# Attention of a hybrid layer: scores with the keys on the partitions, row maxima taken in a pass of their own and fed in as constant rows

## The chip, the cores and the metric

The kernel runs on one core of one Trainium2 chip. The metric is device time in microseconds (us). A core has five engines that work side by side, each through its own list of instructions in a fixed order: PE (TensorE, matrix products and transposes), DVE (VectorE), ACT (ScalarE), POOL (GpSimd) and SP (SyncE, which here only starts DMA transfers). An engine that waits for one instruction holds up everything behind it in its list.

## What is computed

One layer of a streaming encoder on a prompt of 1024 tokens and a block of 32 sample tokens, width 1024. The input is projected, half of the mixing width goes through a state-space branch (S5), the other half through latent attention (MLA) with 8 heads, and both halves meet in one output projection. The part that the change touches:

```python
def mla_attend(q_nope, q_rope, k_nope, k_rope, v, mask):
    s = jnp.einsum('bqhn,bkhn->bhqk', q_nope, k_nope) + jnp.einsum('bqhr,bkr->bhqk', q_rope, k_rope)
    s = s.astype(jnp.float32) * (NOPE_DIM + ROPE_DIM) ** -0.5
    if mask is not None:
        s = jnp.where(mask, s, -jnp.inf)
    pr = jax.nn.softmax(s, axis=-1)
    return jnp.einsum('bhqk,bkhv->bqhv', pr.astype(v.dtype), v)
...
    mix = jnp.concatenate([rmsnorm(y_ssm, p['out_norm_ssm']) * jax.nn.silu(g_ssm),
                           rmsnorm(attn, p['out_norm_mla']) * jax.nn.silu(g_mla)], axis=-1)
    return x + mix @ p['w_out'], ckv, krope, h_last
```

Query q sees key k where the chunk (64 tokens) of q is not before that of k. A head has 64+32 score channels and 64 value channels.

## The kernel before

**Stages.** (1) Input projection (`mt`, L235) with the token norms; (2) the state-space branch; (3) its gate (`gl`); (4) expansion of queries and keys/values for the first four heads (`q_p`, L797 to L799; `kv_p`, L765 to L767); (5) attention; (6) output projection. A scheduler fixes each engine's order when the program is built, from a simulated time line; a tile in a pool of buffers may be written only when the buffer's last reader has gone, so the number of buffers takes part in that order.

**Output projection.** `half(base, ...)` (L855) multiplies one half of the mixed channels by four 128-row blocks of `wout`. Each block is loaded into `wor`, which has two buffers, by a DMA on ACT's queue; `hilo` makes two parts of it, `woh` (ACT) and `wol` (DVE, L113); and the raw block also serves the sample tokens' product `wos` (L863). So the third block's transfer waits until `wos` has read the first. Then each tile of 128 tokens takes 24 products `wo` (L873), 128x512 each: 2 column halves, 4 blocks, 3 parts; 192 for a half. `half(0)` (state-space channels; `out_ssm`, ACT, L885) is a generator that the attention's preamble steps through; `half(4)` (attention channels; `out_y`, DVE, L1184) comes last. `wo` and `wos` take PSUM buffers of tag "w", `q_p`, `kv_p`, the transposes and the value sums those of tag "b" (4).

**Attention.** Heads go in four pairs p; for each pair, 8 query tiles i of 128 (32 units u). `q_tr` transposes the queries, `prep` the keys (`kt_p`). `scores` (L980 to L982) makes [queries on partitions x keys] in three passes (high x high, high x low, low x high); DVE takes the maximum of each row (L989, L1002), ACT the exponential with that as bias and the row sum as accumulated output (L992, L1004). `trans` turns the exponentials into [keys x queries], 128x128 at a time on PE (`pt_p`, L1020, 288 of them); DVE or ACT copies them out of PSUM (L1024, L1026). `values` (L1048) multiplies with the values, 288 products of 128 query columns, each two instructions; the two heads of a pair write two 64-row halves of one PSUM tile. The reciprocal row sums (L1040) are spread by POOL (`rle`, L1042) and transposed by PE (L1049, 32). `finish_at` (POOL) gates, squares and splits the result into `ath` and `atl`. Mask: 8 extra contraction rows, 96 to 103.

**Norms.** `rsqrt` (L151 to L160) is a chain of 11 small DVE instructions; it serves the input norm (`rst`, whose row form `rb` comes out of PE transposes `rb_p`, L185, and scales `uT` at L251), the two branch norms, and the q and kv norms.

Of the kernel before, what the change touches and what calls it, by code (L numbers as in the profile page):

```python
# [24 lines left out]
NT = NP_ + NS  # L25
# [25 lines left out]
def step(ctx: ExitStack, tc, xT, xr, winF, winT, wuq, wukv, wglu, wout, ckvcT, krcT, pk, rot, ssb, ssc, mtab,  # L51
         y_o, ckv_o, kr_o, st_o, dbg=None):
    nc = tc.nc
    pe, act, dve, pool, sp = nc.tensor, nc.scalar, nc.vector, nc.gpsimd, nc.sync

# [106 lines left out]

    def col_rstd(ss, which, name):
# [11 lines left out]
        marks[name] = rsqrt(r, ms, TS)  # L175
# [110 lines left out]
    marks["rst"] = rsqrt(rst, ssx, TS)  # L286
# [568 lines left out]
    def half(base, mix, smp, rstd, out, after, eng=sp):  # L855
        ww = []
        ps = PA("wos", "w")
# [7 lines left out]
        for i0 in range(0, 8, 2):  # L865
            s = {i: [PA("wo", "w") for _ in range(2)] for i in (i0, i0 + 1)}
            mm = {i: mix(i * 128, 128) for i in s}
            for kr in ((0, 1, 2), (3,)) if i0 == 0 else ((0, 1, 2, 3),):
                for i in s:
                    for c in range(2):  # L870
                        for k in kr:
                            for a, b, first, last in ((0, 0, True, False), (0, 1, False, False), (1, 0, False, True)):
                                pe.matmul(s[i][c], mm[i][a][k], ww[k][b][:, c * 512:(c + 1) * 512],  # L873
                                          start=(k == 0 and first), stop=(k == 3 and last))
            if i0 == 0:
                rs = rstd()
                dve.scalar_tensor_tensor(ysm, ps[:, :256], rs[:, 8:9], ysm, op0=MUL, op1=ADD)
            for i in s:
                out(i, s[i], rs[:, i:i + 1])
            yield i0  # L880
# [23 lines left out]

    kT = {}
    KT = {}
    qTh = T("qTh", [104, 10, 256], 1, F32R)
    mk = [T("sg", [128, 1024], 2) for _ in range(2)]
    for j in range(2):
        with tc.issue_after(marks["qe", 0]):  # L910
            act.dma_start(mk[j][96:104], mtab[:, j])
    with tc.issue_after(marks["qe", 1]):
        act.activation(qTh[96:104, 0:8].rearrange("p i (j c) -> p i j c", j=2),
                       mk[0][96:104].rearrange("p (i c) -> p i c", c=128)[:, :, None, :].to_broadcast([8, 8, 2, 128]), AF.Copy)
# [5 lines left out]
    evac = [0]  # L920

    def prep(p, part):
# [3 lines left out]
        if p < 2 and part == 0:  # L926
            KT[p] = T("kTh", [104, 2, 2, 512], 2, F32R), T("kTl", [96, 2, 2, 512], 2, F32R)
        h, lo = (t[:, part] for t in KT[p % 2])
        kT[p, part] = (h, lo)
        if p < 2:  # L930
            src = krT[64:96, None, part * 512:(part + 1) * 512].to_broadcast([DR, 2, 512])
            split(h[64:96], lo[64:96], src, None,  ("qe", 1))
            with tc.issue_after(marks["qe", 1]):
                act.activation(h[96:104], mk[1][96:104, None, part * 512:(part + 1) * 512].to_broadcast([8, 2, 512]), AF.Copy)
# [23 lines left out]
    QT, PR, PTT, RL, OB = {}, {}, {}, {}, {}  # L958

    def q_tr(u):  # L960
        p, i = ORD[u]
# [4 lines left out]
        qh, ql = qTh[:, i], qTh[:96, 8 + u % 2]  # L966
        split(qh[:96], ql, pp[:96, :256], gqk[:96])
        QT[u] = (qh, ql)

    def scores(u):  # L970
        p, i = ORD[u]
        qh, ql = QT.pop(u)
        nb = i + 1
        rl = RL[u] = SM("rl", [4], bufs=4)

        def mm(s, j, c):
            n = min(512, nb * 128 - 512 * c)
            kh, kl = kT[p, c]
            qj = slice(j * 128, (j + 1) * 128)
            pe.matmul(s[:, :n], qh[:, qj], kh[:, j, :n], start=True, stop=False)  # L980
            pe.matmul(s[:, :n], qh[:96, qj], kl[:, j, :n], start=False, stop=False)  # L981
            pe.matmul(s[:, :n], ql[:, qj], kh[:96, j, :n], start=False, stop=True)  # L982

        n = nb * 128
        if i < 4:
# [3 lines left out]
            dve.tensor_reduce(rl[:, 2:4], s[:, :, :n], AX.X, ALU.max, negate=True)  # L989
            t = T("P", [128, 1024], 4)  # L990
            for j in range(2):
                marks["exp", u] = act.activation(t[:, j * n:(j + 1) * n], s[:, j, :n], AF.Exp,  # L992
                                                 bias=rl[:, 2 + j:3 + j], accum_out=rl[:, j:j + 1]).ins
            PR[u] = [t]
        else:
            PR[u] = []
            for j in range(2):
                s = PS2("S")
                for c in range(2):
                    mm(s[:, c], j, c)  # L1000
                sf = s.rearrange("p a b -> p (a b)")[:, :n]
                dve.tensor_reduce(rl[:, 2 + j:3 + j], sf, AX.X, ALU.max, negate=True)  # L1002
                t = T("P", [128, 1024], 4)
                marks["exp", u] = act.activation(t[:, :n], sf, AF.Exp, bias=rl[:, 2 + j:3 + j],  # L1004
                                                 accum_out=rl[:, j:j + 1]).ins
                PR[u].append(t)

    def trans(u):
        p, i = ORD[u]
        nb = i + 1  # L1010
        pr = PR.pop(u)
        out = []
        n = 2 * nb if i < 4 else nb
        for t in pr:
            o = T("PT", [128, 8, 128], 4)
            for b in range(0, n, 4):
                e = min(n, b + 4)
                pp = PA("pt_p", "b")
                for q in range(b, e):
                    pe.transpose(pp[:, (q - b) * 128:(q - b + 1) * 128], t[:, q * 128:(q + 1) * 128], ident)  # L1020
                ov = o[:, b:e].rearrange("p a b -> p (a b)")
                evac[0] += 1
                if evac[0] % 2:
                    dve.tensor_copy(ov, pp[:, :(e - b) * 128])  # L1024
                else:
                    act.activation(ov, pp[:, :(e - b) * 128], AF.Copy)  # L1026
            out.append(o)
        PTT[u] = [(out[0], 0), (out[0], nb)] if i < 4 else [(o, 0) for o in out]

    def values(u):  # L1030
        p, i = ORD[u]
        hf, c0 = p // 2, (p % 2) * 128
        nb = i + 1
        if u % 2 == 0:
            OB[p] = PA("ob", "b")
        ob = OB[p]
        r0 = (i // 4) * 128
        pt = PTT.pop(u)
        rl = RL.pop(u)
        dve.reciprocal(rl[:, 0:2], rl[:, 0:2])  # L1040
        re = T("rle", [128, 128], 2)
        pool.tensor_scalar(re.rearrange("p (a b) -> p a b", a=2), rl[:, 0:2, None].to_broadcast([128, 2, 64]),  # L1042
                           1.0, 0.0, op0=MUL, op1=ADD)
        for q in range(nb):
            for j in range(2):
                v = KV["p", q, hf][:, 256 + c0 + 64 * j:256 + c0 + 64 * j + 64]
                t, b = pt[j]
                pe.matmul(ob[64 * j:64 * j + 64, r0:r0 + 128], v, t[:, b + q], start=(q == 0), stop=(q == nb - 1))  # L1048
        pe.transpose(ob[:, 256 + r0:384 + r0], re, ident)  # L1049
        if u % 2:  # L1050
            bs = T("bs", [128, 256], 2)
# [280 lines left out]
```

## Time and profile before

| what | us |
|---|---|
| three runs | 583.57, 585.41, 587.38 (median 585.41) |
| the profiled execution, its own time | 584.77 |
| its span, first to last instruction | 583.0 |
| around the span (the difference) | 1.77 |
| PE busy | 547.1 (94%) |
| DVE busy | 414.8 (71%) |
| ACT busy | 304.4 (52%) |
| POOL busy | 107.5 (18%) |
| stages: (1) to (3) / (4) / (5), wo mixed in / rest of (6) | 0 to 287 / 287 to 348 / 348 to 540 / 540 to 583 |

PE is nearly always at work, but a stage can have another limit: the profile's table by stretches of time, the chain of work that ended last, and the groups of instructions by line show which. Matmuls overlap, so the price of one is read from the distance between starts, not from its own duration.

### The profile page before, as it was taken

The page shows a single profiled execution, that of the slowest core. Times are in us where ns is not written, and L with a number is a line of the kernel's source. Part 1 is how long each engine was busy: PE and PEld are TensorE (multiplying, and loading weights), DVE is VectorE, ACT ScalarE, POOL GpSimd, SP SyncE. Part 2 cuts the span into 40 slices and gives each one's busy share as a digit, 9 for nine tenths or more (in the row PEclk, how much of TensorE's full clock was granted, in tenths as well). Part 3 has the DMA queues.
Part 4 walks back from the last instruction along what each step waited for, and adds up shares of the span by engine and source line. Part 5 has one row for each costly group of instructions (what it writes and reads, how often), then busy time and mean ns, then how long its engine had stood idle before and what let it go on. Part 6 is the DMA issues. An engine that isn't in the chain of part 4 may idle for free.

```text
span 583.0 us, 9939 instructions
## 1 busy us (share of the span) xinstructions
PE 547.1 (94%) x3707; PEld 481.5 (83%) x3707; DVE 414.8 (71%) x1000; ACT 304.4 (52%) x673; POOL 107.5 (18%) x165
## 2 busy tenths in 40 slices
PE   5989699999999997599999799999999999999997
PEld 5989599899999996599788578877778888877885
DVE  6999722989999254129989986668798577683722
ACT  5571155218135247639855966776676775752000
POOL 0000000000000010000024520222244334468330
PEclk9999799999999998889999899999999999999799
DMA  8991752232433204632401121200100101095352
GB/s 286 405 304 41 199 136 92 49 143 89 130 97 103 66 18 154 201 100 90 141 17 61 43 91 74 92 2 1 38 20 2 38 3 38 7 373 200 104 230 108
DMA packets 35266, 63.92 MB, mean 110 GB/s; under 512 B 5361, under 2 KB 21521, under 8 KB 35217
## 3 DMA queue, kind: packets, MB, share of 16 engines
q1 hardware_dynamic: 31008, 49.06, 25.9%
q10 hardware_dynamic: 4208, 14.22, 6.9%
q8 instruction: 29, 0.48, 0.3%
q14 instruction: 21, 0.16, 0.1%
HBM read 47.06 MB, written 16.21 MB: 109 GB/s over the span
## 4 chain that ended last, share of the span: by engine, by line
PE 74%; DVE 10%; ACT 5%; DMA 5%; issue 2%; POOL 2%; SPq 1%; ACTq 0%; DVEq 0%; POOLq 0%
PE mt L235 24%; PE wo L873 11%; PE ob L1048 6%; PE pt_p L1020 5%; PE S L980 3%; PE S L981 3%; PE S L982 3%; PE tk_p L585 2%; PE tk_p L584 2%; PE tk_p L586 2%; PE gl L705 2%; DMA yg<-dy 1%; PE ob L1049 1%; PE v_p L482 1%; PE qt_p L965 1%
## 5 line engine op out<-in xcount | busy, mean ns | idle before, releaser
L235 PE MATMUL mt<-xh,wh 128*128 128x384 f32 (+1 forms) x288 | 68.5, 335 | 11.9 <-ACT xh L112 6.2
L235 PE MATMUL mt<-xl,wh 128*128 128x384 f32 (+1 forms) x288 | 68.3, 331 | 0.1
L235 PE MATMUL mt<-xh,wl 128*128 128x384 f32 (+1 forms) x288 | 67.3, 330 | 0.0
L235 PEld LDWEIGHTS mt<-xh,wh 128*128 128x128 f32 x288 | 49.8, 193 | 13.5 <-ACT xh L112 6.8
L235 PEld LDWEIGHTS mt<-xl,wh 128*128 128x128 f32 x288 | 49.8, 193 | 1.0 <-issue 0.6
L235 PEld LDWEIGHTS mt<-xh,wl 128*128 128x128 f32 x288 | 49.2, 191 | 0.2 <-issue 0.2
L1020 PE MATMUL pt_p<-base,P 128*128 128x128 f32 x288 | 43.0, 276 | 0.8 <-ACT kv L769 0.7
L1048 PE MATMUL ob<-PT,kv 128*64 128x128 f32 x576 | 41.9, 279 | 0.9 <-DVE PT L1024 0.9
L873 PE MATMUL wo<-woh,mm 128*128 128x512 f32 x128 | 42.0, 398 | 0.3 <-DVE mm L110 0.3
L1048 PEld LDWEIGHTS ob<-PT,kv 128*64 128x64 f32 x576 | 32.0, 136 | 10.3 <-issue 7.2
L736 POOL TENSOR_TENSOR base<-base 128x288 f32<-128x288 f32 x1 | 0.9, 867 | 214.2 <-DVE kro L632 214.2
L1002 DVE TENSOR_REDUCE base<-S 128x1 f32<-128x1024 f32 (+3 forms) x32 | 32.4, 1017 | 10.3 <-PE S L982 10.2
L1004 ACT ACTIVATE P<-S,base 128x1024 f32<-128x1024 f32 (+3 forms) x32 | 30.6, 955 | 15.0 <-DVE base L1002 14.9
L1020 PEld LDWEIGHTS pt_p<-base,P 128*128 128x128 f32 x288 | 33.0, 140 | 5.1 <-ACT kv L769 1.0
L980 PE MATMUL S<-kTh,qTh 104*128 104x512 f32 (+3 forms) x96 | 36.2, 377 | 0.0
L1024 DVE COPY PT<-pt_p 128x512 f32<-128x512 f32 (+2 forms) x44 | 27.9, 635 | 9.3 <-PE pt_p L1020 9.1
L982 PE MATMUL S<-kTh,qTh 96*128 96x512 f32 (+3 forms) x96 | 34.2, 360 | 0.0
L981 PE MATMUL S<-kTl,qTh 96*128 96x512 f32 (+3 forms) x96 | 33.4, 348 | 0.0
L873 PEld LDWEIGHTS wo<-woh,mm 128*128 128x128 f32 x128 | 24.0, 189 | 6.2 <-DVE mm L110 0.7
L109 ACT ACTIVATE wh<-wr 128x512 fp32r<-128x512 f32 x24 | 14.1, 631 | 27.5 <-PE mt L235 25.9
L1184 DVE SCALAR_TENSOR_TENSOR yp<-wo,base,xt 128x512 f32<-128x512 f32 x16 | 11.6, 749 | 21.2 <-PE wo L873 21.2
L819 POOL TENSOR_TENSOR qx<-q,base 128x256 f32<-128x256 f32 (+1 forms) x12 | 8.3, 714 | 98.5 <-ACT q L801 83.0
(346 smaller groups left out, 1443.8 us busy)
## 6 DMA issues: line engine op xcount, KB each, us to landing
wr<-winF SPq DMA_DIRECT2D x10, 512.0 KB, 4.2
U<-du SPq DMA_DIRECT2D x8, 528.0 KB, 4.4
xr<-xr SPq DMA_DIRECT2D x8, 512.0 KB, 7.5
wor<-wout ACTq DMA_DIRECT2D x8, 512.0 KB, 4.3
dyp<-yp SPq DMA_DIRECT2D x8, 512.0 KB, 2.7
part<-dyp ACTq DMA_DIRECT2D x8, 512.0 KB, 5.3
xt<-xr ACTq DMA_DIRECT2D x8, 512.0 KB, 7.2
xr<-xT SPq DMA_DIRECT2D x7, 528.0 KB, 8.1
```

The source lines that it names most:

```text
L109: act.activation(hi, src, AF.Copy)
L235: pe.matmul(ps[c][:, :b - a], ww[:, k, :], xx[k][:, a:b], start=(k == 0 and first), stop=(k == 7 and last))
L584: pe.matmul(p, xhi[k][:, o:o + 128], h, start=(k == 0), stop=False)
L873: pe.matmul(s[i][c], mm[i][a][k], ww[k][b][:, c * 512:(c + 1) * 512], start=(k == 0 and first), stop=(k == 3 and last))
L980: pe.matmul(s[:, :n], qh[:, qj], kh[:, j, :n], start=True, stop=False)
L981: pe.matmul(s[:, :n], qh[:96, qj], kl[:, j, :n], start=False, stop=False)
L982: pe.matmul(s[:, :n], ql[:, qj], kh[:96, j, :n], start=False, stop=True)
L1002: dve.tensor_reduce(rl[:, 2 + j:3 + j], sf, AX.X, ALU.max, negate=True)
L1004: marks["exp", u] = act.activation(t[:, :n], sf, AF.Exp, bias=rl[:, 2 + j:3 + j], accum_out=rl[:, j:j + 1]).ins
L1020: pe.transpose(pp[:, (q - b) * 128:(q - b + 1) * 128], t[:, q * 128:(q + 1) * 128], ident)
L1024: dve.tensor_copy(ov, pp[:, :(e - b) * 128])
L1048: pe.matmul(ob[64 * j:64 * j + 64, r0:r0 + 128], v, t[:, b + q], start=(q == 0), stop=(q == nb - 1))
```

## The change

1. Attention is rewritten around keys on partitions. A first pass (`maxima`) makes only high x high scores with queries on partitions, and DVE takes the row maxima as before. `max_rows` transposes them (4 small PE transposes) and ACT writes them as rows 96 and 97 of the queries' low part `qTl`; the keys carry ones there. `scores` then has the keys stationary and up to 512 query columns moving, so that each result is already [keys x queries], less the maximum; ACT takes the exponential straight into the tile that `values` uses. One step (u, kb) is a half q of a pair's queries (8 units u) and a block kb of 128 keys: 48 steps.
2. The `pt_p` transposes and their copies go. `values` has 96 products of up to 512 columns. Row sums are made by DVE adding the exponential tiles into the unit's first one (40 additions, 16 of 1024 columns, 8 each of 768, 512, 256), and `finish_unit` sums over partitions by a product with ones (`dn`, 16 of 64x512), then a DVE reciprocal of 128x512 and one multiplication. The scores' three passes hold as many columns as before; `maxima` is one more pass.
3. `half` takes PSUM from the two double slots that scores and maxima use, one token tile at a time, and `wos` from tag "b".
4. `rsqrt` for the input norm and the two branch norms becomes one POOL instruction. A memset in a block of its own stands at the start.

```diff
+    with tc.tile_critical():
+        with nc.sbuf_tensor("pad", [128, 2112], F32) as t:
+            nc.gpsimd.memset(t[:, 0:1], 0.0)
...
+    def rsqrt1(y, ms):
+        return pool.tensor_tensor(y, ms, mhalf, op=ALU.pow).ins
...
-    marks["rst"] = rsqrt(rst, ssx, TS)
+    marks["rst"] = rsqrt1(rst, ssx)
...
     def half(base, mix, smp, rstd, out, after, eng=sp):
         ww = []
-        ps = PA("wos", "w")
+        ps = PA("wos", "b")
...
-        for i0 in range(0, 8, 2):
-            s = {i: [PA("wo", "w") for _ in range(2)] for i in (i0, i0 + 1)}
-            mm = {i: mix(i * 128, 128) for i in s}
...
+        for i in range(8):
+            t = PS2("wo")
+            mm = mix(i * 128, 128)
...
+    def max_rows(p, q):
+        rl = RL.pop((p, q))
+        pp = PA("mx_p", "b")
+        for t in range(4):
+            pe.transpose(pp[:2, t * 128:(t + 1) * 128], rl[:, t], ident)
+        for j in range(2):
+            act.activation(qTl[96:98, 4 * q:4 * q + 4, j * 128:(j + 1) * 128],
+                           pp[:2].rearrange("p (t c) -> p t c", t=4), AF.Copy, scale=ident[:2, j:j + 1])
...
+            pe.matmul(sv, kh[:, j, kc], qh, start=True, stop=False)
+            pe.matmul(sv, kl[:, j, kc], qh[:96], start=False, stop=False)
+            pe.matmul(sv, kh[:98, j, kc], ql, start=False, stop=True)
+        t = T("P0", [128, 2, 512], 2) if kb == 0 else T("PT", [128, 2, 512], 4)
+        marks["exp", k] = act.activation(t[:, :, :n], s[:, :, :n], AF.Exp).ins
...
+            s = P0[u][:, :, o:o + n]
+            dve.tensor_tensor(s, s, t[:, :, :n], op=ADD)
+
+    def finish_unit(u):
+        p, q = UN[u]
+        dn = PA("dn", "b")
+        s = P0.pop(u)
+        for j in range(2):
+            pe.matmul(dn[64 * j:64 * j + 64], ones, s[:, j], start=True, stop=True)
+        rc = T("rc", [128, 512], 1)
+        dve.reciprocal(rc, dn)
+        t = T("at", [128, 512], 2)
+        dve.tensor_tensor(t, OB.pop(u), rc, op=MUL)
...
     for i in ssm_half:
-        if i == 4:
+        if i == 5:
             prep(0, 0)
```

**Where instructions stand now.** First PE, in stage (4). Before, the first `wo` of `half(0)` and its `wos` (L863) stand among the `q_p`, and further `wo` fill the list up to the last `kv_p`; 138 of the 192 stand ahead of it. Two pieces of the list before:

```order
L873 MATMUL wo<-woh,mm 128x512
L873 MATMUL wo<-wol,mm 128x512
L863 MATMUL wos<-wor,base 32x256 x4
L171 MATMUL rsy_p<-base,ssy 128x1 x8
...
L873 MATMUL wo<-woh,mm 128x512 x3
L873 MATMUL wo<-wol,mm 128x512
L873 MATMUL wo<-woh,mm 128x512
L765 MATMUL kv_p<-uk,ckh 32x512
```

The end of the same stage in the list of the change (lines have moved: `kv_p` is L775 to L777, `wos` L873, `wo` L882):

```order
L775 MATMUL kv_p<-uk,ckh 32x512
L776 MATMUL kv_p<-uk,ckh 32x512
L777 MATMUL kv_p<-uk,ckl 32x512
L873 MATMUL wos<-wor,base 32x256 x8
L949 MATMUL kt_p<-base,kv 128x128 x4
L981 MATMUL qt_p<-base,q 96x128 x4
L873 MATMUL wos<-wor,base 32x256 x4
L882 MATMUL wo<-woh,mm 128x512 x2
```

All of `wos` now stands behind the last `kv_p`. Only 12 `wo` stand ahead of it, and 180 behind. On ACT, whose queue starts the `wor` transfers, the third and fourth stood between the `q_p` evacuations before, and stand behind the last 128-row `kv_p` evacuation now (`L87 DMA wor<-wout 128x1024 x2`).

Second, DVE in the middle of a pair, here the third one, in the change. The reductions over `wo` are those of `maxima` (L1004; the PSUM slot keeps the name of its first tile), for query tiles 4 to 7:

```order
L1004 TENSOR_REDUCE base<-wo 128x1
L117 SCALAR_TENSOR_TENSOR qTl<-qt_p,base,qTh 96x256
L1004 TENSOR_REDUCE base<-wo 128x1
L1066 RECIPROCAL rc<-dn 128x512
L1004 TENSOR_REDUCE base<-wo 128x1
L1055 TENSOR_TENSOR P_4411<-P_4411,PT 128x2x384
L1004 TENSOR_REDUCE base<-wo 128x1
L1066 TENSOR_TENSOR at<-ob,rc 128x512
L1004 TENSOR_REDUCE base<-wo 128x1
L968 COPY kTs<-kt_p 64x32 x2
L1004 TENSOR_REDUCE base<-wo 128x1 x2
```

The eight reductions of this half stand mixed with two splits of queries, the previous pair's last reciprocal and multiplication, an addition and two copies of sample keys; before, the reductions of a pair are spread over the whole pair, one or two at a time.

Third, PE at the end. Before, 36 `wo` of `half(4)` stand ahead of the sum `rsa_p` that the output's scale needs. In the change 12 do, and `wos` stands behind the last unit's `dn`:

```order
L882 MATMUL wo<-woh,atl 128x512
L180 MATMUL rsa_p<-base,ssa 128x1 x4
L1062 MATMUL dn<-P_4872,base 64x512 x2
L873 MATMUL wos<-wor,base 32x256 x12
L882 MATMUL wo<-woh,ath 128x512 x2
L873 MATMUL wos<-wor,base 32x256 x4
```

So the last 180 `wo` stand behind `wos`, and with it behind the third and fourth `wor`.

At the start, the `rb_p` transposes stand 50 matmuls earlier among the `mt` than before, and on DVE the writing of `uT` has gone ahead with them.

## Rows read from the trace of the kernel before

**Rows 1.** By stretch: start:end, length, busy PE, PEld, DVE, ACT, POOL (instructions), clock, DMA.

```profile
287.00:345.00 58.00, 54.01 (x252) 43.65 (x253) 53.91 (x150) 39.47 (x74) 21.97 (x24) 0.94 0.18 62
...
366.00:400.00 34.00, 33.29 (x272) 27.64 (x272) 25.14 (x53) 23.46 (x60) 9.14 (x18) 1.00 0.10 33
400.00:430.00 30.00, 29.10 (x241) 23.02 (x241) 25.48 (x66) 22.76 (x55) 8.17 (x15) 1.00 0.10 29
430.00:470.00 40.00, 39.95 (x386) 32.61 (x384) 30.02 (x70) 27.35 (x67) 16.71 (x35) 1.00 0.05 15
470.00:512.00 42.00, 42.00 (x413) 35.70 (x413) 30.03 (x60) 26.66 (x66) 17.20 (x37) 1.00 0.10 31
```

**Rows 2.** Chain that ended last, stages (4) to (6): start us, us, what.

```profile
335.73 5.82 PE wo L873 x24
...
352.58 6.47 PE wo L873 x28
...
540.16 38.88 PE wo L873 x156
```

**Rows 3.** Chain, at the start; same columns.

```profile
61.23 4.24 DMA du<-uT
66.10 7.13 PE mt L235 x27
```

**Rows 4.** Time line of PE there: start us, us, engine, what, idle before.

```profile
62.06 0.44 PE L471 MATMUL kp<-base,kst 128*128 128x128 f32 x2 [0.51 <-ACT kst L469]
```

**Rows 5.** DVE by line, 287 to 348: xcount | busy us, mean ns | idle before.

```profile
L110 DVE TENSOR_TENSOR mm<-mix,mm 128x512 fp32r<-128x512 f32 x7 | 4.7, 679 | 0.0
...
L113 DVE SCALAR_TENSOR_TENSOR wol<-wor,base,woh 128x1024 fp32r<-128x1024 f32 x3 | 3.8, 1278 | 0.0
...
L172 DVE TENSOR_SCALAR base<-rsy_p 128x8 f32<-128x8 f32 x1 | 0.2, 168 | 2.1 <-PE rsy_p L170 2.1
```

**Rows 6.** The page's DMA issues: KB each, median us from issue to landing.

```profile
wor<-wout ACTq DMA_DIRECT2D x8, 512.0 KB, 4.3
```

**Rows 7.** ACT by line, 287 to 348.

```profile
L112 ACT ACTIVATE woh<-wor,base 128x1024 fp32r<-128x1024 f32 x2 | 2.4, 1182 | 1.4 <-DMA wor<-wout 1.4
```

**Rows 8.** Chain, attention: starts, us, blocks of one kind.

```profile
366.11 0.90 PE pt_p L1020 x8
370.34 1.90 PE ob L1048 x32
```

**Rows 9.** The page's costliest groups; columns as for DVE by line.

```profile
L1020 PE MATMUL pt_p<-base,P 128*128 128x128 f32 x288 | 43.0, 276 | 0.8 <-ACT kv L769 0.7
...
L1024 DVE COPY PT<-pt_p 128x512 f32<-128x512 f32 (+2 forms) x44 | 27.9, 635 | 9.3 <-PE pt_p L1020 9.1
```

**Rows 10.** Waits, 345 to 512: us in total, times, longest.

```profile
PEld ob L1049 <- issue: 4.3, 25, 0.2
```

**Rows 11.** DVE by line and shape, 340 to 583.

```profile
L1002 DVE TENSOR_REDUCE base<-S 128x1 f32<-128x1024 f32 x8 | 9.6, 1221 | 4.4 <-PE S L982 4.4
...
L113 DVE SCALAR_TENSOR_TENSOR wol<-wor,base,woh 128x1024 fp32r<-128x1024 f32 x4 | 8.4, 2097 | 0.9 <-ACT woh L112 0.9
...
L777 DVE TENSOR_TENSOR kv<-kv,base 128x1024 f32<-128x1024 f32 x6 | 7.5, 1253 | 0.2
...
L1040 DVE RECIPROCAL base<-base 128x2 f32<-128x2 f32 x32 | 5.0, 158 | 11.8 <-ACT P L1004 10.2 <-ACT P L992 1.7
```

**Rows 12.** Time line of DVE, start of the kernel.

```profile
9.28 0.18 DVE L392 TENSOR_TENSOR tmp<-tmp 128x32 f32<-128x32 f32 x1
...
10.29 0.34 DVE L393 RECIPROCAL tmp<-tmp 128x32 f32<-128x32 f32 x1
```

**Rows 13.** Time line of PE, start of the last stage.

```profile
538.05 2.11 PE L170 MATMUL rsa_p<-base,ssa 128*128 128x1 f32 x12 [0.69 <-POOL ssa L1076]
...
540.59 0.63 PE L873 MATMUL wo<-wol,ath 128*128 128x512 f32 x1
...
541.02 0.63 PE L873 MATMUL wo<-woh,atl 128*128 128x512 f32 x1
```

More of the change, by code (lines that the diff above doesn't have):

```diff
@@ L906, in step @@
     KT = {}
-    qTh = T("qTh", [104, 10, 256], 1, F32R)
+    qTh = T("qTh", [106, 8, 256], 1, F32R)
+    qTl = T("qTl", [98, 8, 256], 1, F32R)
+    ones = P("gkv", 0, 64)
+    dve.memset(ones, 1.0)
     mk = [T("sg", [128, 1024], 2) for _ in range(2)]
@@ L919, in step @@
     ssa = T("ssa", [128, TS * 128])
-    evac = [0]
     def prep(p, part):
@@ L988, in scores @@
                 mm(s[:, j], j, 0)
[L989 to L1028, printed above, removed]
@@ L1030, in values @@
-    def values(u):
-        p, i = ORD[u]
-        hf, c0 = p // 2, (p % 2) * 128
[L1033 to L1051, printed above, removed]
-            act.activation(bs, ob[:, 256:512], AF.Copy)
-            d = min(i, 7 - i)
-            t = T("at", [128, 256], 2)
-            dve.tensor_tensor(t, ob[:, 0:256], bs, op=MUL)
-            finish_at(p, slice(d, 8 - d, 7 - 2 * d), t)
+            dve.tensor_reduce(rl, s[:, :, :n], AX.X, ALU.max, negate=True)
@@ new lines, in values @@
+    def values(k):
+        u, kb = STEPS[k]
+        p, q = UN[u]
+        hf, c0 = p // 2, (p % 2) * 128
+        t0, nt, o = span(k)
+        n = nt * 128
+        t = PTS.pop(k)
+        for j in range(2):
+            v = KV["p", kb, hf][:, 256 + c0 + 64 * j:256 + c0 + 64 * j + 64]
+            pe.matmul(OB[u][64 * j:64 * j + 64, o:o + n], v, t[:, j, :n], start=(kb == 0), stop=(kb == 4 * q + 3))
+        if kb:
+            s = P0[u][:, :, o:o + n]
+            dve.tensor_tensor(s, s, t[:, :, :n], op=ADD)
@@ L1137, in sample_c @@
             finish_at(2 * hf + p, None, t)
-    NU = 32
-    ORD = [(p, i) for p in range(4) for d in range(4) for i in (7 - d, d)]
-    EX = (4, 6, 8, 10)
     for i in ssm_half:
-        if i == 4:
+        if i == 5:
             prep(0, 0)
+            for j in range(4):
+                q_tr(0, j)
+            for j in range(4):
+                maxima(0, j)
+            max_rows(0, 0)
             prep(0, 1)
-            q_tr(0)
-            q_tr(1)
-            scores(0)
+            for j in (4, 5, 6):
+                q_tr(0, j)
@@ L1170, in step, with new_pair @@
-    values(NU - 1)
+    def new_pair(p):
+        mla.append(tuple(T("at" + n, [128, NT], 4, F32R) for n in "hl"))
+        GM[p] = LD("gmr", [128, NT], dgm[p], 1, None if p else ("yst", 0, 7))
+    EX = (6, 9, 13, 17)
+    RS = {}
+    for k, (u, kb) in enumerate(STEPS):
+        p, i = k // 12, k % 12
+        scores(k)
+        if i == 0:
+            q_tr(p, 7)
+        if i in (0, 1):
+            maxima(p, 4 + 2 * i)
+            maxima(p, 5 + 2 * i)
+        if i == 2:
+            max_rows(p, 1)
+        if p < 3:
+            if i == 4:
+                prep(p + 1, 0)
+            if 4 <= i < 8:
+                q_tr(p + 1, i - 4)
+            if 5 <= i < 9:
+                maxima(p + 1, i - 5)
+            if i == 9:
+                max_rows(p + 1, 0)
+                prep(p + 1, 1)
+            if i >= 9:
+                q_tr(p + 1, i - 5)
+        if p in (1, 2) and i in (3, 5, 7, 8):
+            (prep_s, sample_a, sample_b, sample_c)[(3, 5, 7, 8).index(i)](p // 2)
+        if k:
+            values(k - 1)
+        if k == 0:
+            new_pair(0)
+        if i == 1 and p:
+            finish_unit(2 * p - 1)
+            new_pair(p)
+        if i == 5:
+            finish_unit(2 * p)
+        if k in EX:
+            expand_kv(1, EX.index(k), ("exp", 0))
@@ L1172, in rsa @@
+    values(len(STEPS) - 1)
+    finish_unit(7)
     def rsa():
@@ L1188, in out_y @@
             sp.dma_start(y_o[i * 128:i * 128 + 128], t)
-    for _ in half(4, lambda o, w: [[t[a][:, o:o + w] for t in mla] for a in range(2)], lambda k: mss[k], rsa, out_y, ("exp", 28), act):
+    for _ in half(4, lambda o, w: [[t[a][:, o:o + w] for t in mla] for a in range(2)], lambda k: mss[k], rsa, out_y, ("exp", 41), act):
         pass
```

127 lines of the change are left out of this document (66 added, 61 removed).

## The prediction

> **What bounds the kernel now.** I read the table by stretches first, to see which engine is full where. In stage (4) both PE and DVE are: 54.01 and 53.91 us busy of 58 [rows 1]. The reader should notice that PE is full there only because output-projection products `wo` fill it: the 138 that the order puts ahead of the last `kv_p` take 138 x 0.231 = 31.9 us, the price being 6.47 us for 28 in the chain [rows 2]. What that stage needs of PE for itself is some 25 us; DVE sets its length. In attention PE is full (144.3 of the 146 us from 366 to 512) and DVE has 110.7 of 146 [rows 1]. The last stage is one run of 156 `wo`, 38.88 us [rows 2]. The chain at the start shows a smaller loss: a transfer of `uT` of 4.24 us from 61.23 is waited for, PE's last work before ends at 62.5, and its `mt` go on at 66.10 [rows 3, 4]. That is 3.6 us of idle PE.
>
> **The change part by part.** The sum is made against the profiled execution, 584.8 us; that is 0.6 under the median.
>
> *Start.* `rb_p` comes 50 matmuls earlier and `uT` with it; 50 `mt` are worth more than the 3.6 us, since 27 of them take 7.13 [rows 3]. The gap should close, and the slow passes behind it too: I take -5, with 0 and -7 as bounds. The memset's block at the start: below nothing it can't go, the nearest wait for a DMA's landing is 4.3 [rows 6], and the first transfer only waits for one tiny POOL instruction; I take +0.5. Together **-4.5**.
>
> *Stage (4) loses its filler.* 126 `wo` (138 less 12) move behind the last `kv_p`: 126 x 0.231 = +29.1. The stage gets shorter only by what DVE loses: four `mm` halves at 0.68, two `wol` at 1.28, the 2.1 us wait for `rsy_p` [rows 5] and half a microsecond for the sample sum: 7.9, say -8. At its end PE does `wos` and must then wait for the third `wor`: 4.3 us of transfer [rows 6] and 1.18 of `woh` [rows 7], +5.5, with only eight transposes to cover it. And PE will have idled half of the stage, so I expect slow passes behind it. The last stage shows their price: its 156 products take 38.88 and not 36.0 at 0.231, and its first ones stand 0.43 apart after PE had waited for `rsa_p` [rows 2, 13]. +2.8. Together **+29.4**. Bounds: 16 for the stage's shortening (if DVE's other instructions there speed up once less runs beside them), 0 for the slow passes, 3 for the wait: +18 to +30.
>
> [...]
>
> *Attention, PE.* Gone: 288 `pt_p` at 0.90/8 = 0.1125 [rows 8, 9], -32.4; 32 `rle` transposes at the same price, -3.6, and the issue gaps of 4.3 us ahead of them [rows 10]. `values` keeps its columns (576 instructions at 1.90/32 = 0.059, 34.2 us [rows 8]) in a sixth of the products; below the present price the columns can't go, so I take -1. New: `maxima`, one pass of the same columns as one of the three now, 48 of 512, 16 each of 384, 256 and 128; by column from 0.231, and not under the 0.1125 of a 128-column transpose, 17.5. `dn`: 16 of 512 columns at four times two `values` instructions, 0.475 each, 7.6. The maxima's transposes: 32 x 0.1125 = 3.6. I add 1.6 for more changes between half-width and full-width products. Net -41.3 + 30.3 = **-11**; bounds -5 (all gaps stay) and -14.
>
> *Attention, DVE.* Gone: 44 copies, 27.9 [rows 9], and 32 reciprocals, 5.0 [rows 11]. New: 40 additions on SBUF of 28,672 columns together. The nearest row is L777, 1.253 for 1024 [rows 11], so 35.1. Eight reciprocals of 128x512 are shown nowhere. One of 128x2 takes 0.158 [rows 11], one of 128x32 0.34, where a product of that size takes 0.18 [rows 12]; from 2 to 32 columns that is 6.1 ns a column, so 3.2 to 3.3 us for 512, 26.7 for the eight. The lower bound is an ordinary 512-column instruction, half of L777 plus its fixed part, 0.75, 6 for the eight. I take 3.3, as only that row is a reciprocal. DVE gets +28.9 net, so from 110.7 to 139.6 in a stretch in which PE now needs 135. DVE becomes the bound of attention, by 4.6 at least.
>
> [...]
>
> *The middle of a pair.* The order makes it worse than the balance. From the first to the last of the eight `maxima` reductions DVE has those (two each of 640 to 1024 columns, by column from 1.221 [rows 11]: 8.1), two query splits (0.95), a reciprocal (3.3), an addition (0.9), the multiplication (0.75) and two copies (0.4): 14.4 us. Only then can `max_rows` run (four transposes and two ACT copies, some 1.7), and behind it stand all scores of the unit q=1. PE has about 11.6 us of other work in that time at the prices above. So 4.5 us of waiting in three pairs (the first pair has `wo` left beside it), 13.5; the balance alone says 4.6. I take **+10**, bounds 0 (cheap reciprocal) and 20 (additions slowed by POOL as `wol` is, 2.10 against 1.28 [rows 5, 11]).
>
> *End.* PE waits for the third `wor` behind `wos`, 5.5 as above; the 2.1 of `rsa_p` and its 0.7 of waiting [rows 13] come under cover, and 2.1 of `wos` moves out of attention: **+0.6**. Nothing else moves there: 180 `wo` are left and not 156, but 12 and not 36 stood earlier.
>
> ACT loses 21 us of PT copies and gets 10 of small ones; it was under PE in every stretch [rows 1], so 0.
>
> Sum: 584.8 - 4.5 + 29.4 - 11 + 10 + 0.6 = **609**.
>
> **The rivals.** *B, DVE is not in the way.* Reciprocals cost 0.75, no wait in the middle of a pair, and stage (4) shortens by 16: 609 - 10 - 8 = 591. For it: the price of the reciprocal is drawn out from 32 columns to 512, and PE had only 54 of 58 in the stage with gaps on all sides. Against: the DVE list holds the reductions behind the reciprocal whatever its price.
>
> *C, the other side: the lost filler costs nothing.* Were stage (4) not set by DVE but by having to do everything on PE, it would shrink by all 29.4, to ACT's length (39.47 less what `half(0)` asks of it), and the rest of the sum gives 584.8 - 4.5 - 11 + 10 + 0.6 = 580, or 570 without the waits. It decides from the point where the deferral costs under 4.9 us, that is, where the stage shrinks to about 34. Against it: DVE is busy for 53.91 of the 58 and loses 8 [rows 1, 5].
>
> *D, half-width products of 512 columns do not overlap by twos.* 0.059 per instruction of 128 columns is a price with the two heads side by side [rows 8]; if the longer ones run one behind the other, `values` and `dn` double: +34 and +7, 650. Against: the pairs are issued as now, one to each half.
>
> *E, DVE and POOL get in each other's way.* Additions and reductions at the slow `wol` price for part of the time: the upper bound of the middles and some more, 620 to 626.
>
> **How the numbers follow.** The sum 0.53, E 0.13, B 0.18, C 0.11, D 0.05. The predicted time is that of the sum. From 589 to 624 the range takes in B, most of E and the bounds of the unknown prices. About 1% (6 us) is what a measurement of this kernel can tell from no change: its runs lie 583.57 to 587.38. Faster by over 1%: C with the waits small, and the low edge of B, 0.11. Within 1%: the upper edge of C and the low edge of B, 0.09. Slower: the rest, 0.80.
>
> **What would show it.** In the changed profile: PE about half idle from 290 to 340, with a low granted clock, `wos` near 335 to 340, a wait of 4 to 6 us behind it, and 130 `wo` in a run; the gap at 62 gone; a reciprocal of 3.3 us; DVE over 90% busy in attention and PE waiting for the reductions at L1004 once a pair; a wait of 5 us ahead of the last `wo` run. It is wrong if stage (4) ends before 325, if the 512-column reciprocal is under 1 us, or if `values` takes more than 40 us.

## The result and the profile after

The changed kernel takes 642.69 us in the median of its runs (635.8 to 646.7), against 584.49 before: 1.096 times as long, with a 95% interval of 1.088 to 1.104. The profiled execution is its fastest, 635.8, with a span of 633.7. The forecast was slower, and it is; but 609 was forecast with 624 as the upper end, so the size was missed by 34 us in the median and by 27 in the profiled execution. All parts below are taken from profiled executions. The medians are of all runs; the ratios leave out runs over 1.5% above a kernel's fastest.

Cut at four places that both kernels have (the gate's first product, the end of the last 128-row `kv_p`, the last `wo` of the first half, the end of the last `values` or `dn`), before and after read so. Table by stretches of the kernel before, with the columns of [rows 1]:

```profile
248.40:348.30 99.90, 94.53 (x480) 80.47 (x481) 85.02 (x192) 69.55 (x129) 21.97 (x24) 0.95 0.23 77
348.30:364.80 16.50, 16.50 (x80) 13.45 (x79) 11.53 (x38) 10.49 (x18) 0.00 (x0) 1.00 0.19 72
364.80:534.70 169.90, 168.17 (x1509) 136.76 (x1507) 127.44 (x267) 112.47 (x271) 68.23 (x120) 1.00 0.18 63
```

and of the changed kernel:

```profile
244.50:327.90 83.40, 65.30 (x325) 57.68 (x329) 71.84 (x155) 56.60 (x109) 22.29 (x24) 0.86 0.14 44
327.90:385.40 57.50, 52.58 (x251) 40.14 (x252) 26.21 (x71) 23.02 (x42) 0.45 (x1) 0.94 0.24 89
385.40:579.80 194.40, 171.34 (x914) 98.48 (x916) 154.08 (x220) 88.06 (x146) 60.65 (x50) 0.95 0.16 57
```

The reader should see three things. The second line has grown from 16.5 to 57.5 us: that is the output projection's first half, now done after the keys and values. The first has shrunk, with PE at 65.30 of 83.40 and a low granted clock. And attention, the third, has PE busy about as long as before (171 against 168) but takes 24.5 us more: PE idles for 23 us in it where it idled for 1.7.

| part | before | after | difference | forecast |
|---|---|---|---|---|
| to the gate's first product | 248.4 | 244.5 | -3.9 | -4.5 |
| gate, stage (4), first half of `wo` | 116.4 | 140.9 | +24.5 | +29.4 |
| attention | 169.9 | 194.4 | +24.5 | -1 |
| rest | 48.3 | 53.9 | +5.6 | +0.6 |

Between the last two lines 16 `wo` and 28 `wos` have changed places: 28 and 32 stood inside attention before, 12 and 4 do now. The `wo` are 3.7 us at the price of [rows 2], the `wos` 1.9 at the 0.067 of their distances between starts. Like for like, attention is +30.1 and the rest 0.0.

### The profile page after: what moved, and what is told of

Read it like the earlier page. It is cut to its first block, busy times and chain, and to the rows that moved or that the text cites. A ratio compares the mean times of both kernels' runs of the same rounds, so it can differ in the third digit from the quotient of the medians.

```text
span 633.7 us, 8579 instructions
## 1 busy us (share of the span) xinstructions
PE 560.1 (88%) x3163; PEld 446.1 (70%) x3163; DVE 442.7 (70%) x933; ACT 278.8 (44%) x549; POOL 110.2 (17%) x99
## 4 chain that ended last, share of the span: by engine, by line
PE 63%; DVE 20%; ACT 7%; issue 5%; DMA 2%; POOL 1%; DVEq 0%; ACTq 0%; POOLq 0%; SPq 0%
PE mt L245 22%; PE wo L882 11%; PE ob L1051 4%; DVE P L1055 3%; PE wo L1032 3%; DVE base L1004 2%; DVE rc L1064 2%; PE tk_p L594 2%; PE tk_p L595 2%; PE wo L1033 2%; PE tk_p L596 2%; PE gl L715 2%; PE wo L1034 2%; PE wo L992 2%; PE dn L1062 1%
## 5 line engine op out<-in xcount | busy, mean ns | idle before, releaser
L1055 DVE TENSOR_TENSOR P<-P,PT 128x1024 f32<-128x1024 f32 (+3 forms) x40 | 43.0, 1074 | 18.3 <-PE ob L1051 10.8
L1036 ACT ACTIVATE PT<-wo 128x1024 f32<-128x1024 f32 (+3 forms) x40 | 30.3, 766 | 51.9 <-PE wo L1034 44.4
L882 PE MATMUL wo<-woh,mm 128*128 128x512 f32 x128 | 42.0, 405 | 2.1 <-ACT mm L113 1.3
L1004 DVE TENSOR_REDUCE base<-wo 128x1 f32<-128x640 f32 (+3 forms) x32 | 32.0, 1014 | 12.7 <-PE wo L992 12.6
L1032 PE MATMUL wo<-qTh,kTh 106*128 106x512 f32 (+3 forms) x96 | 39.3, 409 | 1.6 <-DVE base L1004 1.2
L992 PE MATMUL wo<-kTh,qTh 106*128 106x512 f32 (+3 forms) x96 | 28.2, 380 | 11.4 <-DVE base L1004 3.5
L1033 PE MATMUL wo<-qTh,kTl 96*128 96x512 f32 (+3 forms) x96 | 35.2, 366 | 0.0
L1034 PE MATMUL wo<-qTl,kTh 98*128 98x512 f32 (+3 forms) x96 | 34.7, 365 | 0.0
L1051 PE MATMUL ob<-PT,kv 128*64 128x512 f32 (+3 forms) x160 | 33.5, 499 | 0.8 <-ACT PT L1036 0.8
L882 PEld LDWEIGHTS wo<-woh,mm 128*128 128x128 f32 x128 | 24.6, 193 | 9.0 <-ACT mm L113 1.9
L1064 DVE RECIPROCAL rc<-dn 128x512 f32<-128x512 f32 x8 | 26.8, 3354 | 2.2 <-PE dn L1062 2.0
L882 PE MATMUL wo<-wol,ath 128*128 128x512 f32 x64 | 25.4, 398 | 1.4 <-DVE wol L117 1.4
```

The costliest lines, as they stand in the source:

```text
L882: pe.matmul(t[:, c], mm[a][k], ww[k][b][:, c * 512:(c + 1) * 512], start=(k == 0 and first), stop=(k == 3 and last))
L992: pe.matmul(s[:, :w], qTh[:, i, j * 128:(j + 1) * 128], kT[p, c][0][:, j, :w], start=True, stop=True)
L1004: dve.tensor_reduce(rl[:, j:j + 1], s.rearrange("p a b -> p (a b)")[:, :n], AX.X, ALU.max, negate=True)
L1032: pe.matmul(sv, kh[:, j, kc], qh, start=True, stop=False)
L1033: pe.matmul(sv, kl[:, j, kc], qh[:96], start=False, stop=False)
L1034: pe.matmul(sv, kh[:98, j, kc], ql, start=False, stop=True)
```

## The experiments

All are timed against runs of the kernel before on the same chip (584.8 to 585.1 in the median). In e1, e2, e7 and e11 the memset block has another size, so that the buffers fit; e5 and e6 have no such block. The table has them all, the sections their edits and reasons.

| label | edit | us, median | ratio to before (95%) |
|---|---|---|---|
| | the changed kernel | 642.7 | 1.088 to 1.104 |
| e1_wos_own | `wos` in its own tag | 626.3 | 1.067 to 1.077 |
| e2_no_recip | reciprocal as a copy | 627.4 | 1.068 to 1.076 |
| e3_no_adds | no additions | 627.8 | 1.070 to 1.080 |
| e4_neither | both | 615.3 | 1.048 to 1.055 |
| e5_rsqrt_only | before + POOL inverse roots | 576.2 | 0.983 to 0.990 |
| e6_half_only | before + new `half` | 615.5 | 1.049 to 1.057 |
| e7_own_neither | e1 and e4 | 601.5 | 1.025 to 1.034 |
| e8_no_maxima | no first pass | 599.0 | 1.022 to 1.030 |
| e9_recip_twice | each reciprocal twice | 670.9 | 1.143 to 1.151 |
| e10_adds_split | odd additions on POOL | 645.0 | 1.100 to 1.106 |
| e11_recip_on_act | reciprocal by ACT | 641.1 | 1.082 to 1.094 |
| e12_loads_early | last loads earlier | 636.2 | 1.083 to 1.097 |

### The filler

```diff
-        ps = PA("wos", "b")
+        ps = PA("wos", "w")
```

> The changed kernel with one thing undone: the sample product wos takes PSUM of its own tag again, so that it no longer stands behind all q_p and kv_p in one ring (the memset block at the start is resized to 3432 columns so that the buffers still fit). In the order, 95 wo now stand ahead of the last kv_p (12 in the changed kernel, 138 before), and at the end 12 of the 16 wos stand ahead of the last unit's dn. Theory 1 (what was predicted: the lost filler costs its full length): 83 x 0.231 = 19 us, some 3 of the slow passes behind the idle stretch, and 3 to 5 of the wait ahead of the last wo run come back: 615 to 622. Theory 2 (the filler costs nothing, the whole loss is in attention): 637 to 645.

626.3, 16.4 less than the changed kernel: between the two brackets and nearer to theory 1. In the profiled executions the stages from the gate to the last `wo` of the first half give 17.0 back, where some 22 had been expected, and the end 0.3, where 3 to 5 had: PE idles there for 5.0 us and not 2.2. (Attention is 10 longer in e1's profile, at a granted clock of 0.92; the changed kernel's profiled execution is its fastest, so the medians are the fairer comparison.) 95 `wo` stand under stage (4) again, and the second line of the table by stretches falls from 57.5 to 28.9:

```profile
338.10:367.00 28.90, 27.55 (x135) 21.63 (x133) 14.63 (x44) 13.69 (x26) 0.00 (x0) 1.00 0.22 83
```

The converse, the new `half` put into the kernel before with the old attention (the function's text as in the diff above):

> The kernel before with the change's output projection alone: wo in the two double PSUM slots that the scores use, one token tile at a time, and wos in the ring of tag b; attention is the old one. In the order 12 wo stand ahead of the last kv_p and all wos behind it, as in the changed kernel. Theory 1 (the lost filler is a loss by itself, of some 24 us in the changed kernel's stages): 604 to 612. Theory 2 (it only hurts together with the new attention): 584 to 592.

615.5: 30.7 us lost by this part alone, 3.5 over the bracket. Its first two stretches are those of the changed kernel, its attention that of the kernel before:

```profile
249.80:333.40 83.60, 65.68 (x325) 57.71 (x325) 72.08 (x161) 58.21 (x111) 18.77 (x20) 0.86 0.13 43
333.40:392.20 58.80, 50.92 (x243) 39.19 (x243) 25.56 (x71) 22.94 (x38) 2.71 (x5) 0.94 0.25 91
392.20:559.40 167.20, 164.80 (x1476) 134.34 (x1475) 123.19 (x262) 109.92 (x268) 68.01 (x119) 1.00 0.15 55
```

So more than half of the change's loss needs no new attention at all: behind the sample product's place in a ring of buffers wait the third and fourth weight block, and behind those 126 products that had filled PE's idle time. Of the 126, e1 brings back 83, and 17.0 of the 24.5 us, by that place alone. The other 43 and their 7.5 us e1 leaves; `half` in the two double PSUM slots, another part of e6, was not tried by itself.

### DVE's list in attention

```diff
-        dve.reciprocal(rc, dn)
+        dve.tensor_copy(rc, dn)
```

> The changed kernel with the eight 128x512 reciprocals replaced by plain copies of the same size (the sums are then not inverted; the memset block is 3168 columns so that the buffers fit). A copy of this size takes 0.68, the reciprocal 3.35: 21 us less DVE work. Theory 1 (DVE's list holds PE in the middle of a pair and behind the last unit, the reciprocal being 3.4 of some 14 us there): PE's waits at the maxima shrink by about 2.7 in each of three pairs and at both ends of the last pair: 625 to 633, and a higher granted clock in attention. Theory 2 (the waits come from two PSUM slots shared by maxima and scores, whatever DVE does in between): 637 to 645.

> The changed kernel without the 40 additions of exponential tiles (the denominators then hold the first key block alone). 43 us less DVE work. Theory 1 (DVE's list holds PE): the last unit's run of additions, ahead of which PE stands idle for some 9 us at the end, goes, and the waits in the middle of the pairs shrink: 618 to 628. Theory 2 (PSUM slots): only the end's 9 us come back: 632 to 636.

> The changed kernel with neither the additions nor the reciprocals (copies in their place): 64 us less DVE work. Theory 1 (DVE's list holds PE): nearly all idle time of PE between the first scores and the last dn goes (22 us) and the slow passes behind it: 608 to 618, with the stage before attention unchanged. Theory 2 (PSUM slots): PE still stands at the maxima for a third and more of its idle time: 626 to 634.

627.4, 627.8 and 615.3. Taking 21 us off DVE gives 15 back, 43 us give 15, both together give 27. All three are in the bracket of "DVE's list holds PE". In the third, attention reads:

```profile
385.70:558.40 172.70, 164.07 (x938) 97.32 (x936) 101.96 (x183) 88.38 (x146) 49.35 (x52) 0.98 0.17 61
```

PE's idle time falls from 23.1 to 8.6, the stages ahead of it stay as they were, and the granted clock rises to 0.98. Without the DVE work the rival (two PSUM slots shared by maxima and scores) can claim no more than these 8.6, of which 5.4 lie directly behind maxima and their transposes. With it the two are not separate, since a slot with maxima is held until DVE has reduced it; what a third slot would save there was not tried. The dose in the other direction:

```diff
         dve.reciprocal(rc, dn)
+        dve.reciprocal(rc, dn)
```

> The changed kernel with each of the eight reciprocals done twice: 26.8 us more DVE work at the places where a copy in its place (21.4 us less) gave 15 of 642.7 back. In the order of PE and DVE hardly a row moves. Theory 1 (DVE's list holds PE at these eight places, and each us of it there costs 0.7): 656 to 664. Theory 2 (the gain of the copy came from another order or from the clock, and DVE has room): 640 to 648.

670.9, +28.2 for 26.8 us of DVE work, more than the bracket. In the profiled executions attention takes 31 more and what follows it 7; in attention PE, with the same instructions, is busy 20 us longer:

```profile
383.80:609.40 225.60, 191.27 (x906) 109.09 (x908) 177.12 (x227) 89.26 (x146) 55.98 (x50) 0.84 0.14 47
```

PE idles for 34 us here, 11 more than in the changed kernel, and the granted clock is 0.84 where that one has 0.95. So the added work shows twice, as waiting and as slower passes, and each us of it costs 1.05, against 0.7 where the reciprocals were taken away. The 20 us are an upper bound for the slower passes, since the changed kernel's profiled execution is its fastest by 6 to 11 us.

Two attempts to take the work off DVE without leaving it out:

```diff
-            dve.tensor_tensor(s, s, t[:, :, :n], op=ADD)
+            (pool if kb % 2 else dve).tensor_tensor(s, s, t[:, :, :n], op=ADD)
```

> The changed kernel with every second addition of exponential tiles on POOL (odd key blocks), the same work otherwise. DVE loses some 22 of 43 us, POOL gets some 45 on its 60 in attention, and the two engines work on SBUF side by side more often. Leaving all additions out gave 15 back. Theory 1 (DVE's length alone matters): half of that, 632 to 638. Theory 2 (DVE and POOL slow each other: DVE's additions took 1.42 in the mean against 1.25 for L777, and 1.86 each while POOL worked at the end): no gain or a loss, 643 to 660.

645.0, not told apart from the changed kernel: theory 1 is out. By line, 380 to 640:

```profile
L1055 POOL TENSOR_TENSOR P<-P,PT 128x1024 f32<-128x1024 f32 x8 | 19.0, 2372 | 35.0 <-PE ob L1051 21.5 <-DVE P L1055 9.6 <-ACT PT L1036 3.9
L1055 DVE TENSOR_TENSOR P<-P,PT 128x1024 f32<-128x1024 f32 x8 | 11.7, 1464 | 2.7 <-ACT PT L1036 2.7
L1062 PE MATMUL dn<-P,base 128*64 128x512 f32 x32 | 10.2, 722 | 7.5 <-POOL P L1055 7.5
```

An addition on POOL is longer (2.37 us), and the additions of a unit are one chain through P0, whichever engine does them; PE now waits for POOL ahead of `dn`.

```diff
-        dve.reciprocal(rc, dn)
+        act.activation(rc, dn, AF.Ln)
+        act.activation(rc, rc, AF.Exp, scale=-1.0)
```

> The changed kernel with the reciprocal made by ACT, as the exponential of the negative logarithm (two ACT instructions on 128x512, some 0.7 each, and table loads where the tables differ), DVE without it; the memset block is 3168 columns. ACT is busy for 88 of 194 in attention. Theory 1: as with copies on DVE, a little better for the DVE time and a little worse for ACT's tables: 624 to 632. Theory 2 (the table loads of 1.28 us each stand in the way of the exponentials): 636 to 645.

641.1, in theory 2's bracket; the ratio, 1.088, has an interval that overlaps with the changed kernel's, so no gain can be told from none. Logarithm and exponential were given different tables, and each unit pays two loads:

```profile
L1064 ACT ACT_TABLE_LOAD x8 | 10.3, 1283 | 7.6 <-PE dn L1062 7.1 <-DVE P L1055 0.4
L1065 ACT ACT_TABLE_LOAD x8 | 10.3, 1283 | 0.1
```

With its own two instructions a unit's reciprocal takes 3.8 us of ACT, no less than the 3.35 on DVE, and the exponentials of the next steps stand behind it.

### PE's own sum

> The changed kernel with wos in its own PSUM tag and without additions and reciprocals, so with the filler and without the DVE work that the rewrite brought (it leaves out the sums over the other key blocks and the inversion). 615.3 was measured without the two, and 16 of 642.7 came back with the tag. If the two are independent: 597 to 602. If the rewrite's PE work alone is as predicted (11 less than before) it has to come out 11 to 15 below the kernel before, 570 to 575; if PE's work is unchanged by the rewrite, at 585 plus what 43 wo less ahead of kv_p and the waits at the maxima cost, 592 to 600.

(the edits of e1 and e4 together). 601.5, at the upper end of the bracket for "independent" and far from the 570 to 575 that the forecast's PE term would need. It is close to the upper end of "PE's work is unchanged", 592 to 600, too. With most of the filler back and without 64 us of DVE work, the kernel is still 2.9% slower than before: the stages from the gate to the last `wo` of the first half take 7.0 us more, and PE idles for 10.1 us in attention where it idled for 1.7:

```profile
369.90:543.80 173.90, 163.79 (x942) 96.74 (x940) 103.21 (x185) 88.97 (x147) 49.44 (x52) 0.99 0.17 61
```

```diff
-            if 5 <= i < 9:
-                maxima(p + 1, i - 5)
             if i == 9:
-                max_rows(p + 1, 0)
                 prep(p + 1, 1)
...
```

> The changed kernel without its first pass: no maxima products, no row reductions and no transposes of the maxima; the constant rows of the queries' low part hold one number for all queries (it leaves out the row maxima). It measures what the first pass costs as a whole. PE loses 22 us of maxima and 3 of transposes, DVE 45 of reductions. Theory 1 (DVE's list holds PE in attention): with DVE at some 110 of 170 there, the idle time at the maxima (some 14) and most of the slow passes go as well: 596 to 604. Theory 2 (PE's sum decides, DVE's reductions stand beside it): 25 to 28 less, 615 to 618.

599.0: 43.7 us for the first pass as a whole, within theory 1. PE's busy time in attention falls by some 31, DVE's by 33, and the clock comes back:

```profile
383.50:539.00 155.50, 140.67 (x800) 81.21 (x802) 121.30 (x176) 78.08 (x132) 61.14 (x51) 0.98 0.21 76
```

One number for all queries is no replacement for row maxima in general, since exponentials can leave the range; the run prices the pass and no more.

### The start, and the end

```diff
-        marks[name] = rsqrt(r, ms, TS)
+        marks[name] = rsqrt1(r, ms)
...
-    marks["rst"] = rsqrt(rst, ssx, TS)
+    marks["rst"] = rsqrt1(rst, ssx)
```

> The kernel before with one part of the change alone: the three inverse square roots (input norm, two branch norms) as one POOL instruction each in place of DVE's chain of 11; no memset block. In the order rb_p stands 33 matmuls earlier, and the filler of stage (4) stays (140 wo ahead of the last kv_p). In the changed kernel the gate's first product starts 3.9 us earlier than before. Theory 1 (that gain is the inverse square root's, and nothing later eats it): 579 to 582. Theory 2 (the gain at the start comes from the other reordering, or is lost to waits later): 584 to 586.

576.2, 1.4% faster than before, better than the bracket, and the fastest kernel of this study. The gate's first product starts at 242.2 and not 248.4, attention is as long as before to the tenth of a us, and the rest is 1.5 shorter, with PE busy 1.4 less at a granted clock, up to its last product, of 0.96 and not 0.92; why was not taken apart.

```profile
0.00:242.20 242.20, 220.63 (x1462) 211.78 (x1462) 171.53 (x465) 111.16 (x255) 5.67 (x11) 0.99 0.48 152
358.30:528.20 169.90, 168.01 (x1507) 136.62 (x1506) 127.52 (x266) 112.22 (x271) 68.00 (x120) 1.00 0.17 62
```

This is the one part of the change that was found to gain.

```diff
-            with tc.issue_after(marks["exp", 41]):
+            with tc.issue_after(marks["exp", 30]):
```

> The changed kernel with one number moved: the loads of the last half's weights, of the partial sums and of the residual may start behind step 30's exponential instead of step 41's. In DVE's order the first two wol splits then stand some 28 rows earlier, ahead of the last two units' reciprocals, and POOL can add the residual tiles earlier. In the changed kernel's profile PE idles for some 9 us ahead of the last dn, while DVE does a reciprocal, two wol (3.3 and 1.3), and six additions of which five take 1.86 each beside POOL. Theory 1 (that idle stretch is this collision): 4 to 8 of it come back, 634 to 639. Theory 2 (the work only moves, and collides earlier with the same weight): 640 to 646.

636.2, but the intervals overlap, and the profiled execution is no shorter (a span of 635.6 against 633.7): inconclusive. The two `wol` now stand before those reciprocals, and `dn` no longer follows on the last addition: that one ends at 576.0, and the last reciprocal, at 580.25, has waited 4.25 us for `dn`. But PE idles for 22.0 us in attention where it idled for 23.1, and is busy 2.6 longer at a granted clock of 0.93. An addition of 128x768 takes 1.84 at 549.58, where the mean in the changed kernel is 1.06; why was not taken apart.

## Why the prediction went wrong

**Right.** *The start*: -3.9 for -4.5, and e5 shows whose it is. The gap of 3.6 us at 62 is gone; one of 2.1 stands at 59 in its place. *The lost filler*: +24.5 for +29.4 in the changed kernel, +26.0 in the same stages of e6. `wos` came at 328 to 337 (335 to 340 had been named), 130 `wo` followed in one run, and PE's clock was low in the stage (0.86). Stage (4) shrank by 16.5 and not 8, the bound that had been named for it, but not for the reason named: DVE is busy 13.2 us less in it and idle only 3.3 less. Besides `mm` and `wol`, some 7 us of a `kv` block's norm now stand behind the last `kv_p`, and the branch norm's 2.7 are POOL's. (The lower bounds of this term add up to 16, not to the 18 given.) *The reciprocal*: 3.3 us had been drawn out from 32 columns. From the page:

```profile
L1064 DVE RECIPROCAL rc<-dn 128x512 f32<-128x512 f32 x8 | 26.8, 3354 | 2.2 <-PE dn L1062 2.0
```

That is 6.55 ns a column, 5.4 times the 1.22 of L777 [rows 11]. *The middle of a pair* has the order that was described; the chain of the changed kernel shows it, in the last pair:

```profile
532.95 3.36 DVE rc L1064
536.30 0.81 DVE base L1004
537.12 0.86 DVE P L1055
537.97 1.00 DVE base L1004
538.98 0.60 DVE at L1066
539.57 2.14 DVE base L1004 x2
541.76 0.48 PE wo L1032
```

Reductions, reciprocal, addition and multiplication stand one behind the other, and only behind the last reduction can the scores run. *The rivals*: B falls by the reciprocal's price and e9, C by e6, D by `values`, whose 192 instructions of up to 512 columns take 39.3 us where the 576 of 128 took 39.2. (Both by distances between starts; the prediction's 34.2 came from one block of the chain and was too low for the whole.) E's 620 to 626 is too low as well.

**Wrong: the step "Attention, PE", net -11.** It measured about 0: without the DVE work, in e4, PE is busy 164.1 us in attention, 8 `wo` (1.8) among them, against 168.2 before with 28 `wo` (6.5), and 32 `wos` in both: 162.2 against 161.7. Term by term from the distances between starts: the `pt_p` gave their 32, `dn` and the maxima's transposes took 11 as priced. But the `rle` transposes gave 4.6 with all their gaps and not 7.9, since the issue gaps had been counted on top of a distance that held them. And all 96 `maxima` took 23.3 and not 17.5. They had been priced as passes within a run. A time line of e4 shows what a first product costs:

```profile
466.56 0.50 PE L1032 MATMUL wo<-qTh,kTh 106*128 106x512 f32 x1
466.90 0.40 PE L1033 MATMUL wo<-qTh,kTl 96*128 96x512 f32 x1
467.13 0.40 PE L1034 MATMUL wo<-qTl,kTh 98*128 98x512 f32 x1
```

The first pass, here behind half-width products, starts its successor 0.34 later, the second 0.23. Each tile of maxima is two products, the first of them mostly such a first one: the 48 of 512 columns took 14.4 and not 11.1, the 48 narrower ones 8.9 and not 6.4. Scores lose about 2 in the same way.

**Wrong: "+10" for the middles as all the waiting in attention.** PE idles for 23.1 us in attention and not for 1.7: +21. The middles cost 2 to 4 us each, less than the 4.5 worked out, but in all four pairs, the first among them, and not in three: some 11 together, so that their +10 came out near by luck. The other half lies where the sum had nothing. DVE was not over 90% busy, as had been expected of the bound of attention, but 79% (154.1 of 194.4), and PE 88%: each waits for the other in turn. And DVE had more to do, as the 40 additions took 43.1 us and not 35.1:

```profile
L1055 DVE TENSOR_TENSOR P<-P,PT 128x1024 f32<-128x1024 f32 x16 | 22.8, 1422 | 13.6 <-PE ob L1051 10.8 <-ACT PT L1036 2.7
L1055 DVE TENSOR_TENSOR P<-P,PT 128x768 f32<-128x768 f32 x8 | 8.5, 1058 | 0.1
L1055 DVE TENSOR_TENSOR P<-P,PT 128x512 f32<-128x512 f32 x8 | 6.4, 797 | 3.3 <-ACT PT L1036 3.2
L1055 DVE TENSOR_TENSOR P<-P,PT 128x256 f32<-128x256 f32 x8 | 5.4, 671 | 1.3 <-ACT PT L1036 1.0
```

The end of attention was left out, where the additions of the last unit run behind two `wol` and beside POOL's residual tiles. The chain there:

```profile
560.58 1.02 DVE wol L117
561.60 2.19 issue
563.79 3.40 DVE P L1055
...
570.22 1.89 DVE P L1055
572.20 1.86 DVE P L1055
574.16 1.59 DVE P L1055
575.84 2.39 DVE P L1055
578.37 1.45 PE dn L1062 x4
```

An addition that takes 1.23 alone (at 555.66) takes up to 3.40 while POOL adds `xt`; PE does its 12 `wo` meanwhile and then stands 3.0 us for `dn`. The prediction had this as rival E's price and gave it no place in the sum. Another 5 us of idle time lie between query transposes and what follows them, and some 4 in short waits; they were not taken apart.

**Missing: slow passes inside attention.** The sum had them behind stage (4) alone. In the changed kernel attention runs at full clock up to 530, and then:

```profile
385.40:530.00 144.60, 129.04 (x747) 76.09 (x746) 118.77 (x195) 73.42 (x129) 38.96 (x38) 1.00 0.06 19
530.00:579.80 49.80, 42.30 (x168) 22.39 (x171) 35.32 (x26) 14.64 (x19) 21.69 (x12) 0.82 0.46 165
```

The low clock lies behind the waits of the last pair's middle, where PE was busy 3.0 of 5 us:

```profile
535.00:540.00 5.00, 2.99 (x11) 1.17 (x11) 5.00 (x6) 0.50 (x1) 0.28 (x1) 1.00 0.00 0
540.00:545.00 5.00, 3.99 (x16) 3.04 (x16) 2.83 (x3) 0.23 (x1) 4.75 (x5) 0.64 0.00 0
545.00:558.00 13.00, 11.89 (x30) 5.73 (x31) 3.04 (x4) 4.98 (x7) 0.40 (x1) 0.50 0.30 113
558.00:575.00 17.00, 17.00 (x81) 9.70 (x80) 16.69 (x9) 5.90 (x7) 11.47 (x5) 0.99 0.76 268
```

The time line of PE has passes 0.43 apart there in place of 0.23:

```profile
549.27 0.63 PE L1034 MATMUL wo<-qTl,kTh 98*128 98x512 f32 x1
549.70 0.63 PE L1032 MATMUL wo<-qTh,kTh 106*128 106x512 f32 x1
550.13 0.63 PE L1033 MATMUL wo<-qTh,kTl 96*128 96x512 f32 x1
```

The granted clock is 0.50 over these passes (549 to 552) and 1.00 from 410 to 420, where passes stand 0.23 apart. The kernel before has the same pair: 0.43 apart at 0.50 from 540.6 to 545 [rows 13], and 0.23 apart at 1.00 in the 28 `wo` of [rows 2]. PE's busy time, less the 12 `wo` and 4 `wos`, is 168.1, 8 us over that of e4 without its 8 and 32. The other runs of the changed kernel show a granted clock of 0.933 to 0.940 where the profiled one has 0.954, and are 6 to 11 us longer.

**Luck: the end.** +0.6 was forecast and 0.0 like for like came, but not by the terms: behind `wos` PE waits 1.4 us, and for `wol`, where 5.5 for the third `wor` had been worked out.

Together: PE's sum +11.5, waits +11.4, slow passes +8, less 5 for the deferral, while start and end cancel: 26 of the 27 us between 609 and 635.8. The first is a price: short groups were priced as a run. The other two are one omission: in a stage that two engines share, what one waits for was priced in one place and taken as free in the others.

## What to carry to other kernels

A product that fills another engine's waiting was worth nearly its whole length here (83 of 0.231, 19.2 us, brought 17.0 back in e1): before a buffer ring or tag is shared, look at what stands ahead in the ring and what waits behind. When a rewrite takes work from the engine that is full and gives it to one that is busy three quarters of the time (DVE, 110.7 of 146 us [rows 1]), add up the second one first: the gain was nil on PE and the loss came with DVE's additions, the reciprocal and the first pass's reductions. And a change made of parts is worth taking apart, as the one small edit that gains here (1.4%) was hidden under two that lose.

## What the runs showed of the hardware

- A reciprocal of 128x512 on DVE takes 3.35 us. Against the 0.34 of 32 columns [rows 12] that is 6.3 ns for each further column, near the 6.1 between 2 [rows 11] and 32.
- A product of 512 columns starts its successor 0.31 to 0.34 us later when it follows a transpose or a half-width product, 0.23 to 0.24 within a run or behind a `kv_p` of the same width (e4, and the changed kernel up to 530); so short groups of mixed kinds are dearer than their columns.
- More waiting on PE in attention went with a lower granted clock: at 8.6, 23.1 and 34.3 us of idle time it was 0.98, 0.95 and 0.84 (e4, the changed kernel, e9). It does not follow from the sum of the waits alone: e1 has 0.92 at 22.3 and e10 0.90 at 26.0, and the changed kernel's own waits left the clock at 1.00 up to 530. Why stays open.
- A DVE addition of 128x1024 took 1.2 to 3.4 us, the longest beside POOL's work on 128x1024; on POOL it took 2.37.
